# 16-bit projections, the first pair's values and the dilation-4 table loaded beside the last projection job, and another order between the two mixers of a Hymba-style encoder block

## The chip, the cores and the metric

The kernel runs on one core of one Trainium2 chip. The metric is the device time of one execution in microseconds. TensorE (PE) multiplies matrices, VectorE (DVE), ScalarE (ACT) and GpSimd (POOL) work on elements, and SyncE (SP) issues most DMAs.

## The reference

One encoder block over 2048 tokens of 1024 numbers, in float32. What matters here is its first half:

```python
h = rmsnorm(x, g_attn_norm[l])
proj = h @ w_in[l]                     # 1024 -> 3*512 + 256 + 128 + 32
q_a, k_a, v_a, c_q, c_kv, k_rope = jnp.split(proj, splits, axis=-1)
out_a = mixer_dilated(heads(q_a), heads(k_a), heads(v_a), rel_bias)   # 8 heads of 64
out_b = mixer_mla(c_q, c_kv, k_rope, g_q_latent[l], w_q_up[l], g_kv_latent[l], w_kv_up[l])
```

`mixer_dilated` attends in three windows, with keys 1, 4 and 16 tokens apart and a bias by distance for each, and joins them by their softmax denominators. `mixer_mla` is attention over low-rank latents. Behind it come the output projection with a residual, a mixture of 32 experts, and a last norm; the change does not touch these.

## The kernel before

**Number format.** Each projection is computed three times over: both operands are split into a high part and the residual (`hT_hi`, `hT_lo`; `w_hi`, `w_lo` or `wc_hi`, `wc_lo`), and hi x hi, lo x hi and hi x lo are summed in PSUM. The parts are fp32r, a 32-bit format that TensorE takes as it is; the trace prints its matmuls as f32. `split` (L98) does it with one ScalarE copy and one VectorE subtraction.

**Phase 1** (L83). `stage_a` norms a tile of 128 tokens, `stage_b` transposes it on TensorE into `hT`, and `stage_c` multiplies it with the 416 latent columns (24 matmuls). The loop over 16 tiles also lets helpers (Python generators) advance a step at a time: `bias_tables` (L410) builds the bias tables from one-hot matrices, which it keeps in the last 768 columns of `hT_hi`, and `vscale` (L229) finds a power of two by which v fits fp16: Squares of the weights, a ones-matmul that sums over partitions (L350), and some ten tiny VectorE operations (`pow2_scale`, L344). `gmax` is the largest g_attn.

Then come six jobs. The two "v" jobs do 16 tiles of 256 columns each (L309, evicted at L316). The four "qk" jobs do 8 groups each of 24 matmuls of 512 tokens (L329); each group is evicted as an fp16 high part and its residual (`qk_sb`, L339 and L340, two buffers each) and stored to DRAM by two DMAs on SP (L342). At the start of each job the weights of the next are split, with `qkscale` for its scale; `v_copies` makes rearranged copies of v in DRAM (`v1`, `v1e`, `v4`, `v4e`) beside the qk jobs. At the start of the last job `pre3` (L456) asks for head 0's q and k and for the bias tables `t16` and `t1` (the page calls all tables t).

**Phase 3** (L513), the dilated attention, loads the values of head pair 0 (L545) and the table `t4` (L579), scales the three tables on GpSimd (`scale_tables`, L572), and goes through 160 steps: scores on TensorE (L645), `soft1` on VectorE (L670), `soft2` on GpSimd (L687), the exponential on ScalarE (L697), transposes on TensorE (L710), then the product with v.

**mla_prep** (L1006) prepares mixer B: its weights `wkv` are split, `stage_a1` norms a tile's latents (L1036), `stage_a2` transposes them, `stage_b` multiplies and writes the values `VB` (L1079). `qk_scales` (L793) finds the scale of its scores by a ones-matmul (L799) and a VectorE chain.

The order on each engine is that in which the code is written; waits are set by what reads and writes which buffer. PSUM tile `pm` has four buffers.

## Time and the profile before

| | us |
|---|---|
| median of 3 executions | 2322.38 (2321.01 to 2323.44) |
| the profiled execution | 2328.61 |
| its span, first to last instruction | 2326.8 |
| TensorE / VectorE / ScalarE / GpSimd busy in it | 2077.9 / 1653.5 / 1426.9 / 1093.3 |

The profiled execution's time stands 1.8 us above its span: that is what lies around the first and last instruction. Busy times are those of the hardware profiler. In the rows further below a row of a timeline begins with its start and its length in us; "x8" are instructions taken together, and the bracket gives how long the engine stood idle before and what ended that. The mean granted clock of TensorE was 0.948 of its full rate.

### The profile page before, as it was taken

The numbers are of one execution on the slowest core, as the hardware profiler recorded it, in microseconds if no ns is written. First come the engines' busy times: TensorE is split into PE (matmuls) and PEld (weight loads), VectorE is DVE, ScalarE is ACT, GpSimd is POOL, SyncE is SP. The second block draws the span as 40 slices with busy tenths as digits, with TensorE's granted clock in tenths as the row PEclk, the third lists the DMA queues.
The fourth block names the chain that finished last, engine by engine and source line by source line (L and its number), as shares of the span: only waits on it lengthen the run. The fifth ranks groups of instructions, "written<-read, shape, count | busy, mean of one in ns | idle before, by whom it ended". The sixth has DMA issues, their size and how long they took to land. (4 is left out here: it accounts for less than half of the span.)

```text
span 2326.8 us, 42792 instructions
## 1 busy us (share of the span) xinstructions
PE 2077.9 (89%) x16087; PEld 1584.7 (68%) x16087; DVE 1653.5 (71%) x3656; ACT 1426.9 (61%) x2121; POOL 1093.3 (47%) x1193
## 2 busy tenths in 40 slices
PE   6899989688988899999999999788888899999990
PEld 5899778577777556656656555477776588788870
DVE  7722221388886888888888899967787677777755
ACT  4522211399996588888888878734443366677653
POOL 1100000278763255555555556644564656776640
PEclk9999999899998899999999999999998999999995
DMA  5412434867735100000000231145544689999978
GB/s 163 126 58 62 144 140 112 178 156 170 160 99 139 48 22 6 22 22 6 22 22 6 45 102 26 34 135 160 151 143 158 205 307 292 293 307 313 305 212 306
DMA packets 196676, 312.81 MB, mean 134 GB/s; under 512 B 64185, under 2 KB 149090, under 8 KB 183460
## 3 DMA queue, kind: packets, MB, share of 16 engines
q1 hardware_dynamic: 166420, 174.43, 26.2%
q0 software_dynamic: 29760, 134.85, 18.0%
q8 instruction: 127, 2.08, 0.4%
q10 hardware_dynamic: 288, 0.79, 0.1%
q14 instruction: 81, 0.66, 0.1%
HBM read 235.66 MB, written 101.25 MB: 145 GB/s over the span
## 5 line engine op out<-in xcount | busy, mean ns | idle before, releaser
L923 POOL TENSOR_TENSOR lo<-p,hi 128x512 f16<-128x512 f32 x256 | 342.7, 1343 | 297.3 <-ACT p L917 235.5
L916 ACT ACTIVATE hi<-S,mla_scale 128x1024 f16<-128x1024 f32 x256 | 285.2, 1114 | 136.2 <-PE S L911 134.7
L885 DVE TENSOR_REDUCE part<-M 128x1 f32<-128x512 f32 x512 | 340.4, 680 | 12.8 <-PE M L883 11.5
L917 ACT ACTIVATE p<-S,mla_scale 128x1024 f32<-128x1024 f32 x256 | 284.8, 1113 | 0.1
L922 DVE TENSOR_TENSOR lo<-p,hi 128x512 f16<-128x512 f32 x256 | 228.7, 894 | 11.3 <-ACT p L917 9.5
L945 PE MATMUL O<-VB,lo 128*128 128x65 f16 x2048 | 198.4, 194 | 7.6 <-DVE lo L922 5.3
L940 PEld LDWEIGHTS <-hi 128*128 128x128 f16 x2048 | 184.6, 98 | 28.0 <-issue 22.7
L940 PE MATMUL O<-VB,hi 128*128 128x129 f16 (+1 forms) x2048 | 198.5, 215 | 0.0
L945 PEld LDWEIGHTS <-lo 128*128 128x128 f16 x2048 | 177.5, 99 | 18.0 <-DVE lo L922 6.4
L693 POOL TENSOR_TENSOR pp<-sb,st 128x256 f32<-128x256 f32 (+1 forms) x256 | 142.6, 579 | 43.3 <-DVE st L670 30.5
L572 POOL TENSOR_SCALAR t<-t,a_scale 128x512 f32<-128x512 f32 (+1 forms) x12 | 16.1, 1351 | 305.1 <-DMA t<-d_r 290.9
L2077 DVE TENSOR_TENSOR s<-raw,s 128x1024 fp32r<-128x1024 f32 x120 | 140.2, 1221 | 15.0 <-ACT s L2075 13.8
L2121 POOL DMA_INDIRECT d_x<-o,rec x47 | 94.0, 2000 | 107.3 <-ACT s L2075 35.5
L710 PE MATMUL PT<-ident,pp 128*128 128x128 f32 (+1 forms) x640 | 104.3, 287 | 43.8 <-ACT pp L697 41.5
L2034 PE MATMUL pd<-s,hT 128*128 128x512 f32 x540 | 138.2, 404 | 1.7 <-ACT hT L2021 1.7
L1385 PE MATMUL pm<-s,mT_hi 128*128 128x512 f32 x512 | 136.1, 413 | 3.8 <-ACT mT_hi L1370 3.8
L340 DVE SCALAR_TENSOR_TENSOR qk_sb<-pm,qkscale,qk_sb 128x512 f16<-128x512 f32 x32 | 23.9, 750 | 152.5 <-ACT qk_sb L339 152.5
L697 ACT ACTIVATE pp<-pp,a_scale 128x512 f32<-128x512 f32 (+1 forms) x160 | 113.8, 711 | 29.3 <-POOL pp L687 19.8
L2075 ACT ACTIVATE s<-raw 128x1024 fp32r<-128x1024 f32 x120 | 118.3, 1050 | 11.5 <-DMA raw<-in_w_up,eidx 4.7
L2034 PEld LDWEIGHTS pd<-s,hT 128*128 128x128 f32 x540 | 101.2, 188 | 30.1 <-issue 4.3
L339 ACT ACTIVATE qk_sb<-pm,qkscale 128x512 f16<-128x512 f32 x32 | 21.9, 687 | 161.8 <-PE pm L329 110.4
L1385 PEld LDWEIGHTS pm<-s,mT_hi 128*128 128x128 f32 x512 | 98.1, 197 | 26.0 <-ACT mT_hi L1370 4.1
(502 smaller groups left out, 6081.2 us busy)
## 6 DMA issues: line engine op xcount, KB each, us to landing
x<-in_x SPq DMA_DIRECT2D x32, 512.0 KB
na<-d_na SPq DMA_DIRECT2D x48, 264.0 KB
d_qk<-qk_sb SPq DMA_DIRECT2D x64, 128.0 KB
d_x<-x SPq DMA_DIRECT2D x16, 512.0 KB
d_h<-h SPq DMA_DIRECT2D x16, 512.0 KB
y<-d_x SPq DMA_DIRECT2D x16, 512.0 KB
out<-y SPq DMA_DIRECT2D x16, 512.0 KB
d_q<-qs SPq DMA_DIRECT2D x16, 384.0 KB
```

The lines of the kernel that those rows point to most:

```text
L693: nc.gpsimd.tensor_sub(dst, src, res[:, s0 + i, 65:66, None, None].to_broadcast([128, 2, na, nx // 2]))
L885: nc.vector.tensor_reduce(part[m][:, qt, kc:kc + 1], ps, axis=AX.X, op=ALU.max)
L916: nc.scalar.activation(hi, ps, AF.Exp, scale=es)
L917: nc.scalar.activation(p32, ps, AF.Exp, scale=es)
L922: nc.vector.tensor_sub(lo[:, :, 0:LV], p32[:, :, 0:LV], hi[:, :, 0:LV])
L923: nc.gpsimd.tensor_sub(lo[:, :, LV:512], p32[:, :, LV:512], hi[:, :, LV:512])
L940: nc.tensor.matmul(o[:, c0:c0 + own], hi[:, j, q], V[:, 0:own], start=(kt == 0 and qt == 0), stop=False, skip_group_check=True)
L945: nc.tensor.matmul(o[:, c0:c0 + 65], lo[:, j, q], V[:, 0:65], start=False, stop=(kt == 15 and qt == 3), skip_group_check=True)
L1385: nc.tensor.matmul(ps[half], mT[a][:, j], wo[b][j // 2][:, j % 2, 512 * half:512 * half + 512], start=(n == 0), stop=(n == 23))
L2034: self.nc.tensor.matmul(ps[:, half], hT[a][:, j], w[b][:, j, 512 * half:512 * half + 512], start=(n == 0), stop=(n == len(k) - 1))
L2075: nc.scalar.activation(hi, src, AF.Copy)
L2077: eng.tensor_sub(lo, src, hi)
```

## The change

(1) `hT`, `wc` and the split weights are fp16. As fp16 reaches less far than fp32r, the operands are multiplied by powers of two before the split and the results by the inverse on eviction: `xs` for h comes from gmax at the very start, and `weight_scale` gives one for each weight block (`wsc`). The latent weights' scale needs a Square over both halves ahead of the first split. `vscale` and `qkscale` get a second ones-matmul and chain each, and `qkscale` runs whole at the job's start. (2) The one-hot matrices have a tile of their own. (3) `pre3` also makes room for the first pair's values and `t4`; a generator `ahead3` asks for them, a step in each group of the last job, and only `t16` is scaled ahead of the first attention step, `t1` and `t4` at steps 1 and 9. (4) In `mla_prep` the split of `wkv` stands behind the first `stage_a2`, its Square behind the second, and `qk_scales` behind the second `stage_b`.

The diff, cut to what bears on this:

```diff
-            hT = [hp.tile([128, 8, S], F32R, name="hT_hi"), hp.tile([128, 8, S], F32R, name="hT_lo")]
+            hT = [hp.tile([128, 8, S], F16, name="hT_hi"), hp.tile([128, 8, S], F16, name="hT_lo")]
+
+            xs = hp.tile([128, 2], F32, name="hscale")
+            wsc = [hp.tile([128, 3], F32, name=f"wscale{i}") for i in range(3)]
...
-            def split(hi, lo, src):
-                nc.scalar.activation(hi, src, AF.Copy)
-                nc.vector.tensor_sub(lo, src, hi)
+            def split(hi, lo, src, sc):
+                nc.scalar.activation(hi, src, AF.Copy, scale=sc)
+                nc.vector.scalar_tensor_tensor(lo, src, sc, hi, op0=ALU.mult, op1=ALU.subtract)
+
+            def weight_scale(am, w, out):
+
+                nc.vector.memset(am[:, 2:3], 1.0)
+                yield from self.pow2_scale(sm, pt, am, 1.0, w[:, 0:1], None, w[:, 1:2])
+                nc.vector.tensor_scalar(w[:, 2:3], w[:, 1:2], xs[:, 1:2], out, op0=ALU.mult, op1=ALU.mult)
...
-                split(wcv[0][:, 4 * h:4 * h + 4], wcv[1][:, 4 * h:4 * h + 4], wraw[h])
+                split(wcv[0][:, 4 * h:4 * h + 4], wcv[1][:, 4 * h:4 * h + 4], wraw[h], wsc[2][:, 0:1])
...
+            am = sm.tile([128, 4], F32, name="vmax")
+            nc.vector.tensor_reduce(am[:, 2:3], gb, axis=AX.X, op=ALU.max, apply_absolute_value=True)
+            nc.vector.tensor_copy(gmax, am[:, 2:3])
+            self.pow2(sm.tile([128, 8], F32, name="p2"), gmax, gmax, float(D), xs[:, 0:1], xs[:, 1:2])
             stage_a(0)
+            am = sm.tile([128, 4], F32, name="vmax")
+            for h in range(2):
+                nc.scalar.activation(wcv[h][:, 0:4], wraw[h], AF.Square, accum_out=am[:, h:h + 1])
+            list(weight_scale(am, wsc[2], 1.0))
             split_c(0)
             stage_b(0)
             split_c(1)
...
-                nc.vector.tensor_reduce(am[:, 2:3], gb, axis=AX.X, op=ALU.max, apply_absolute_value=True)
-                nc.vector.tensor_copy(gmax, am[:, 2:3])
-                nc.vector.tensor_copy(self.mam[:, 5:6], am[:, 2:3])
+                nc.vector.tensor_copy(am[:, 2:3], gmax)
+                nc.vector.tensor_copy(self.mam[:, 5:6], gmax)
                 yield
                 yield from self.pow2_scale(sm, pt, am, float(D), vsc, dr["va_inv"])
+                a2 = sm.tile([128, 4], F32, name="vmax")
+                nc.vector.tensor_copy(a2[:, 0:2], am[:, 0:2])
+                yield from weight_scale(a2, wsc[0], vsc)
...
+                yield from weight_scale(a2, wsc[g % 2 + 1], s2[:, 0:1])
...
-            tables = self.bias_tables(rawp, hT[0][:, :, 1280:2048], tb)
+            tables = self.bias_tables(rawp, xp.tile([128, 4, 768], F32R, name="onehot", bufs=1), tb)
...
-                if c in (10, 11, 12, 13, 14):
+                if c >= 9:
                     next(vs, None)
+                    if c >= 13:
+                        next(vs, None)
...
                     self.pre3()
+                    a3 = self.ahead3()
                 if i + 1 < len(jobs):
                     if jobs[i + 1][0] == "qk":
-                        qs_steps = qkscale(i + 1)
-                        next(qs_steps)
+                        for _ in qkscale(i + 1):
+                            pass
...
-                        nc.scalar.activation(vt[:, :, 0:64], pv, AF.Copy, scale=vsc)
-                        nc.vector.scalar_tensor_tensor(vt[:, :, 65:129], pv, vsc, vt[:, :, 0:64],
+                        nc.scalar.activation(vt[:, :, 0:64], pv, AF.Copy, scale=wsc[0][:, 2:3])
...
+                            if i == len(jobs) - 1:
+                                next(a3, None)
+                            s2 = wsc[g % 2 + 1][:, 2:3]
...
+        self.pre2 = self.c_pre.enter_context(tc.tile_pool(name="p3pre2", bufs=1, side="right"))
+        self.c_v = ExitStack()
+        pv = self.c_v.enter_context(tc.tile_pool(name="p3pv", bufs=1, side="right"))
+        self.v0 = lambda: pv.tile([128, 63, 2, VW], F16, name="v0")
+        self.t4 = pv.tile([128, 8, 256], F32, name="t4")
...
+    def load_v(self, p, t):
+
+        nc, dr = self.nc, self.dram
+        R = 8 * VW
+        f = t.rearrange("p b h n -> p b (h n)")
+        for n, b0, nb, src in ((128, 0, 16, "va"), (128, 16, 15, "v1"), (96, 31, 4, "v1e"), (128, 35, 12, "v4"), (96, 47, 16, "v4e")):
+            nc.sync.dma_start(f[:n, b0:b0 + nb], AP(dr[src], p * 2 * VW, [[R, n], [n * R, nb], [1, 2 * VW]]))
+            if src != "v1":
+                yield
+
+    def ahead3(self):
+
+        nc, dr = self.nc, self.dram
+        self.v_first = self.v0()
+        yield from self.load_v(0, self.v_first)
+        for a in range(4):
+            nc.sync.dma_start(self.t4[32 * a:32 * a + 32].rearrange("p h (a x) -> p (h a) x", a=4),
+                              AP(dr["r4"], a * 3072, [[1, 32], [96, 32], [1, 64]]))
+            yield
 
...
-            def scale_tables(g):
-                for t in (t16, t1, t4):
+            def scale_tables(g, ts):
+                for t in ts:
                     nc.gpsimd.tensor_scalar(t[:, 2 * g:2 * g + 2], t[:, 2 * g:2 * g + 2], self.asc[:, g, 0:1], None, op0=ALU.mult)
 
-            t4 = tp.tile([128, 3072], F32, name="t4")[:, 0:2048].rearrange("p (h x) -> p h x", h=8)
-            vl = load_v(0)
-            next(vl)
-            next(vl)
-            for a in range(4):
-                nc.sync.dma_start(t4[32 * a:32 * a + 32].rearrange("p h (a x) -> p (h a) x", a=4),
-                                  AP(dr["r4"], a * 3072, [[1, 32], [96, 32], [1, 64]]))
-            list(vl)
-            scale_tables(0)
+            t4 = self.t4
+            vs[0] = self.v_first
+            scale_tables(0, (t16,))
...
+                    if s in (1, 9):
+                        scale_tables(0, (t1,) if s == 1 else (t4,))
...
-        nc.scalar.activation(wkv[1][:, :, 0:64], raw2[:, :, 0:64], AF.Square, scale=gkv, accum_out=self.mam[:, 2:3])
-        nc.scalar.activation(wkv[0], raw2, AF.Copy, scale=gkv)
-        nc.vector.scalar_tensor_tensor(wkv[1], raw2, gkv, wkv[0], op0=ALU.mult, op1=ALU.subtract)
...
-        self.qk_scales(self.sm4, pt)
         stage_a2(0)
+        nc.scalar.activation(wkv[0], raw2, AF.Copy, scale=gkv)
+        nc.vector.scalar_tensor_tensor(wkv[1], raw2, gkv, wkv[0], op0=ALU.mult, op1=ALU.subtract)
         for c in range(NT):
             if c + 2 < NT:
                 stage_a1(c + 2)
             if c + 1 < NT:
                 stage_a2(c + 1)
+            if c == 0:
+                nc.scalar.activation(raw2[:, :, 0:64], raw2[:, :, 0:64], AF.Square, scale=gkv, accum_out=self.mam[:, 2:3])
             stage_b(c)
+            if c == 1:
+                self.qk_scales(self.sm4, pt)
```

Three places where the order of instructions on an engine differs. First, ScalarE at the start of the program (`raw` holds the halves of the latent weights, `xn` a tile of x, `pT` its transposes). Before:

```order
L141 ACTIVATE xn,ss<-x 128x1024
L99 ACTIVATE wc_hi<-raw 128x1664
L187 ACTIVATE c_junk,mla_norms<-raw 128x128
L160 ACTIVATE hT_hi<-pT 128x4x128 x2
L99 ACTIVATE wc_hi<-raw 128x1664
L187 ACTIVATE c_junk,mla_norms<-raw 128x128
```

After the change:

```order
L150 ACTIVATE xn,ss<-x 128x1024
L207 ACTIVATE wc_hi,vmax<-raw 128x1664
L207 ACTIVATE wc_lo,vmax<-raw 128x1664
L102 ACTIVATE wc_hi<-raw,wscale_114 128x1664
L196 ACTIVATE c_junk,mla_norms<-raw 128x128
L102 ACTIVATE hT_hi<-pT,hscale 128x4x128 x2
L102 ACTIVATE wc_hi<-raw,wscale_114 128x1664
L196 ACTIVATE c_junk,mla_norms<-raw 128x128
```

Two Squares (L207) now stand ahead of the first cast of the weights, and both casts read the scale that comes of them. Second, SP's queue of DMAs in the last projection job (`t_...<-d_t` is t1, `qk_sb` are the stores of the groups, `v` the values of the first pair, `t_...<-d_r_66` is t4). Before, t1 is followed by the sixteen stores, and at their end stands:

```order
L342 DMA d_qk<-qk_sb_3445 128x512
L342 DMA d_qk<-qk_sb_3446 128x512
L545 DMA v<-d_va 128x16x260
L545 DMA v<-d_v_59 128x15x260
L545 DMA v<-d_v1e 96x4x260
L579 DMA t_3485<-d_r_66 32x32x64 x4
L545 DMA v<-d_v_61 128x12x260
L545 DMA v<-d_v4e 96x16x260
```

After the change, from t1 on:

```order
L500 DMA t_3301<-d_t_65 8x8x256 x16
L508 DMA v_3353<-d_va 128x16x260
L367 DMA d_qk<-qk_sb_3355 128x512
L367 DMA d_qk<-qk_sb_3356 128x512
L508 DMA v_3353<-d_v_59 128x15x260
L508 DMA v_3353<-d_v1e 96x4x260
L367 DMA d_qk<-qk_sb_3388 128x512
L367 DMA d_qk<-qk_sb_3389 128x512
L508 DMA v_3353<-d_v_61 128x12x260
L367 DMA d_qk<-qk_sb_3420 128x512
L367 DMA d_qk<-qk_sb_3421 128x512
L508 DMA v_3353<-d_v4e 96x16x260
```

The five loads of v stand ahead of the stores of the first four groups, in one of them two together; the four loads of t4 stand likewise, one ahead of the stores of each of the last four groups. Behind the stores there is nothing left to load for the first pair. Third, ScalarE between the mixers, from the last results of the dilated attention (`st`) on (`t` holds the weights of wkv, `wq_raw` the latents of the first tiles, `css` their norms). Before:

```order
L752 ACTIVATE st_8241<-O 128x4x65
L1025 ACTIVATE s_9377,mla_norms<-t_8854,glat 128x8x64
L1026 ACTIVATE s_9377<-t_8854,glat 128x1024
L1036 ACTIVATE cn<-wq_raw,css 128x256
L1037 ACTIVATE cn<-wq_raw,css 128x128
L1036 ACTIVATE cn<-wq_raw,css 128x256
L1037 ACTIVATE cn<-wq_raw,css 128x128
L1048 ACTIVATE cqT_hi<-pT 128x256
```

After the change, from the second tile's norms on:

```order
L1071 ACTIVATE cn<-wq_raw,css 128x256
L1072 ACTIVATE cn<-wq_raw,css 128x128
L1083 ACTIVATE cqT_hi<-pT 128x256
L1084 ACTIVATE s_9493<-pT 128x128
L1150 ACTIVATE s_9495<-t_8972,glat 128x1024
L1071 ACTIVATE cn<-wq_raw,css 128x256
L1072 ACTIVATE cn<-wq_raw,css 128x128
L1083 ACTIVATE cqT_hi<-pT 128x256
L1084 ACTIVATE s_9493<-pT 128x128
L1158 ACTIVATE t_8972,mla_norms<-t_8972,glat 128x8x64
L1104 ACTIVATE qs<-pq 128x8x64
L1114 ACTIVATE VB<-pv,vb_scale 128x8x64
```

The Square (with the tile that sums it, `mla_norms`) and the split of wkv stood first; now two tiles' norms (L1071, L1072) and the first tile's transposes stand ahead of the split, and the Square stands just ahead of the first tile's results.

## Rows read from the trace of the kernel before

**Rows 1.** The page: busy us, share of the span, instructions by engine.

```profile
PE 2077.9 (89%) x16087; PEld 1584.7 (68%) x16087; DVE 1653.5 (71%) x3656; ACT 1426.9 (61%) x2121; POOL 1093.3 (47%) x1193
```

**Rows 2.** Windows: length; PE, PEld, DVE, ACT, POOL busy; clock; DMA share; GB/s.

```profile
30.00:92.00 62.00, 55.48 (x283) 48.88 (x282) 45.07 (x133) 26.96 (x75) 9.54 (x48) 0.92 0.38 111
...
233.00:383.00 150.00, 140.28 (x588) 114.15 (x589) 29.29 (x70) 26.44 (x36) 0.00 (x0) 0.94 0.36 130
...
394.00:404.00 10.00, 10.00 (x45) 8.21 (x44) 0.47 (x1) 0.00 (x0) 0.93 (x1) 1.00 0.60 79
...
428.00:436.00 8.00, 1.59 (x26) 1.29 (x23) 2.62 (x24) 1.18 (x3) 0.00 (x0) 0.81 1.01 250
436.00:444.00 8.00, 0.00 (x0) 0.00 (x0) 0.00 (x0) 0.00 (x0) 0.00 (x0) 0.50 1.34 178
```

**Rows 3.** Timeline of the start.

```profile
9.32 1.59 ACT L99 ACTIVATE wc_hi<-raw 128x1664 fp32r<-128x1664 f32 x1 [2.02 <-DMA raw<-in_w_in]
...
12.83 1.75 PE L168 MATMUL pm<-wc_hi,hT_hi 128*128 128x416 f32 x4
```

**Rows 4.** Timeline of VectorE, tiles 12 and 13: maximum; first and last of a chain.

```profile
113.55 1.21 DVE L235 TENSOR_REDUCE vmax<-g_attn 128x1 f32<-128x1024 f32 x1
...
128.21 0.15 DVE L352 COPY p<-pT 128x2 f32<-128x2 f32 x1
...
129.68 0.14 DVE L364 TENSOR_SCALAR p<-p 128x1 int32<-128x1 int32 x1
```

**Rows 5.** Timeline of TensorE in the loop over tiles.

```profile
48.99 0.42 PE L434 MATMUL pT<-hT_hi 33*8 33x496 f32 x1 [0.98 <-ACT hT_hi L160]
...
95.19 1.77 PE L168 MATMUL pm<-wc_hi,hT_hi 128*128 128x416 f32 x8
...
99.83 1.03 PE L158 MATMUL pT<-ident,xn 128*128 128x128 f32 x8
...
115.67 0.58 PE L350 MATMUL pT<-vmax,ones 128*128 128x2 f32 x2 [3.93 <-DVE hT_lo L161]
```

**Rows 6.** Timeline of TensorE in mixer B, 16-bit operands.

```profile
899.69 0.38 PE L910 MATMUL S<-Ql,Kh 96*128 96x512 f16 x1
...
900.56 0.38 PE L910 MATMUL S<-Ql,Kh 96*128 96x512 f16 x1
```

**Rows 7.** Timeline of ScalarE: evictions of value and q/k jobs.

```profile
201.21 0.47 ACT L316 ACTIVATE v_sb<-pm,va_scale 128x256 f16<-128x256 f32 x1 [2.25 <-PE pm L309]
...
252.13 0.69 ACT L339 ACTIVATE qk_sb<-pm,qkscale 128x512 f16<-128x512 f32 x1 [4.81 <-PE pm L329]
...
332.14 0.69 ACT L339 ACTIVATE qk_sb<-pm,qkscale 128x512 f16<-128x512 f32 x1 [7.38 <-DMA d_qk<-qk_sb]
...
410.96 1.27 ACT L339 ACTIVATE qk_sb<-pm,qkscale 128x512 f16<-128x512 f32 x2 [17.28 <-DMA d_qk<-qk_sb]
```

**Rows 8.** Timelines of TensorE, SP and GpSimd from the last job on.

```profile
381.81 1.99 PE L329 MATMUL pm<-hT_hi,wc_hi 128*128 128x512 f32 x8
...
388.27 15.24 SPq L467 DMA_DIRECT2D t<-d_t  x16
...
427.48 0.22 PE L645 MATMUL S<-KA,QA 128*128 128x128 f16 x1 [1.56 <-DVE qk_sb L340]
...
446.38 1.56 POOL L572 TENSOR_SCALAR t<-t,a_scale 128x512 f32<-128x512 f32 x1 [33.74 <-DMA t<-d_r]
447.90 4.06 POOL L687 TENSOR_TENSOR pp<-sb,st 128x512 f32<-128x512 f32 x4
...
449.76 1.11 PE L710 MATMUL PT<-ident,pp 128*128 128x128 f32 x4 [19.93 <-ACT pp L697]
```

**Rows 9.** Timelines of ScalarE and TensorE between the mixers.

```profile
706.01 0.72 ACT L1025 ACTIVATE s<-t,glat 128x512 fp32r<-128x512 f32 x1 [6.48 <-DMA d_na<-st]
...
706.88 0.60 PE L799 MATMUL pT<-mla_norms,ones 128*128 128x6 f32 x2 [7.77 <-ACT s L1025]
...
716.56 0.69 ACT L1079 ACTIVATE VB<-pv,vb_scale 128x512 f16<-128x512 f32 x1 [0.52 <-PE pv L1066]
```

More of the change, by code (lines that the diff above doesn't have):

```diff
@@ L125, in phase1 @@
             nc.scalar.dma_start(gb, AP(io["g_attn_norm"], 0, [[0, 128], [1, D]]))
-            wc = [wp.tile([128, 8 * 416], F32R, name="wc_hi"), wp.tile([128, 8 * 416], F32R, name="wc_lo")]
+            wc = [wp.tile([128, 8 * 416], F16, name="wc_hi"), wp.tile([128, 8 * 416], F16, name="wc_lo")]
             wcv = [t.rearrange("p (j n) -> p j n", j=8) for t in wc]
@@ L171, in stage_c @@
                 cj = cev.tile([128, 256], BF16, name="c_junk")
-                nc.scalar.activation(cj, ps[:, 0:256], AF.Square, accum_out=self.css[:, 0, c:c + 1])
-                nc.scalar.activation(cj[:, 0:128], ps[:, 256:384], AF.Square, accum_out=self.css[:, 1, c:c + 1])
+                o = wsc[2][:, 2:3]
+                nc.scalar.activation(cj, ps[:, 0:256], AF.Square, scale=o, accum_out=self.css[:, 0, c:c + 1])
+                nc.scalar.activation(cj[:, 0:128], ps[:, 256:384], AF.Square, scale=o, accum_out=self.css[:, 1, c:c + 1])
                 cs = cev.tile([128, 416], F32, name="c_sb")
-                nc.scalar.activation(cs, ps[:, :416], AF.Copy)
+                nc.scalar.activation(cs, ps[:, :416], AF.Copy, scale=o)
                 t = cev.tile([128, 4, 16], F32, name="c_rope")
@@ L212, in split_job @@
                     if 0 not in sps:
-                        sps[0] = [sps["pool"].tile([128, 2048], F32R, name="w_hi"),
-                                  sps["pool"].tile([128, 2048], F32R, name="w_lo")]
+                        sps[0] = [sps["pool"].tile([128, 2048], F16, name="w_hi"),
+                                  sps["pool"].tile([128, 2048], F16, name="w_lo")]
                     w = sps[0]
@@ L219, in split_job @@
                 r = raws.pop(i)
+                sc = wsc[0 if kind == "v" else g % 2 + 1][:, 0:1]
                 if kind == "v":
-                    split(w[0], w[1], r)
+                    split(w[0], w[1], r, sc)
                 else:
@@ L249, in qkscale @@
                 s2 = sq[g % 2]
+                a2 = sm.tile([128, 4], F32, name="vmax")
+                nc.vector.tensor_copy(a2[:, 0:2], am[:, 0:2])
                 yield from self.pow2_scale(sm, pt, am, float(D), s2[:, 0:1], None, s2[:, 1:2], low=16.0)
+                yield from weight_scale(a2, wsc[g % 2 + 1], s2[:, 0:1])
                 a = self.asc[:, g]
@@ L334, in phase1 @@
                                 next(vc, None)
-                            if hh == 0 and n4 in (1, 3):
-                                next(qs_steps, None)
-                            s2 = sq[g % 2][:, 0:1]
+                            if i == len(jobs) - 1:
+                                next(a3, None)
+                            s2 = wsc[g % 2 + 1][:, 2:3]
                             qs = [qkp.tile([128, 512], F16, name=f"qk_sb{t}") for t in range(2)]
@@ L367, in pow2_scale, with pow2 @@
         yield
+    def pow2(self, m, u, v, k, scale, inv, low=1e-30):
+        V = self.nc.vector
+        V.scalar_tensor_tensor(m[:, 0:1], u, k, v, op0=ALU.mult, op1=ALU.mult)
+        V.tensor_scalar(m[:, 1:2], m[:, 0:1], low, 1e30, op0=ALU.max, op1=ALU.min)
+        mi = m.bitcast(I32)
+        V.tensor_scalar(mi[:, 1:2], mi[:, 1:2], 1, None, op0=ALU.logical_shift_right)
+        V.tensor_scalar(mi[:, 1:2], mi[:, 1:2], float(127 << 22), None, op0=ALU.add)
+        V.tensor_single_scalar(mi[:, 2:3], mi[:, 1:2], 0x7F800000, op=ALU.bitwise_and)
+        V.tensor_scalar(scale.bitcast(I32), mi[:, 2:3], -1.0, float((127 + 14 + 127) << 23), op0=ALU.mult, op1=ALU.add)
+        V.tensor_scalar(mi[:, 3:4] if inv is None else inv.bitcast(I32), mi[:, 2:3], -float(14 << 23), None, op0=ALU.add)
     def v_copies(self):
@@ L540, in load_v @@
             def load_v(p):
-                R = 8 * VW
-                t = vp.tile([128, 63, 2, VW], F16, name="v")
-                f = t.rearrange("p b h n -> p b (h n)")
-                def ld(np_, b0, nb, src):
-                    nc.sync.dma_start(f[:np_, b0:b0 + nb], AP(src, p * 2 * VW, [[R, np_], [np_ * R, nb], [1, 2 * VW]]))
-                vs[p] = t
-                ld(128, 0, 16, dr["va"])
-                yield
-                ld(128, 16, 15, dr["v1"])
-                ld(96, 31, 4, dr["v1e"])
-                yield
-                ld(128, 35, 12, dr["v4"])
-                ld(96, 47, 16, dr["v4e"])
+                t = vs[p] = self.v0() if p % 2 == 0 else vp.tile([128, 63, 2, VW], F16, name="v")
+                for _ in self.load_v(p, t):
+                    pass
             def vblk(pat, w, half):
@@ L772, in phase3 @@
                     if u == 5 and h % 2 == 0 and h // 2 + 1 < 4:
-                        list(load_v(h // 2 + 1))
+                        load_v(h // 2 + 1)
                     if u == 12 and h % 2 and h // 2 + 1 < 4:
-                        scale_tables(h // 2 + 1)
+                        scale_tables(h // 2 + 1, (t16, t1, t4))
+                    if s in (1, 9):
+                        scale_tables(0, (t1,) if s == 1 else (t4,))
                     qk(s)
```

28 lines of the change are left out of this document (8 added, 20 removed).

## The prediction

> **What bounds the kernel now.** I read the page first, then the busy times by stretch, then the timelines of the stretches that the diff touches. TensorE is busy 2077.9 us, 89% of the span [rows 1], so in most places what counts is how long its stream is and where it stands still. The stretch table shows which is which: from 233 to 383 us it is busy 94% of the time, VectorE and ScalarE less than a quarter of it; in 394 to 404 it never rests, with the DMA engines 60% busy; from 436 to 444 no compute engine does anything, the DMA engines are full and the granted clock is 0.50, which is 1.2 of 2.4 GHz [rows 2]. So there are four kinds of ground: a start ruled by loads and ScalarE, a projection loop in which TensorE, ScalarE and VectorE take turns, projection jobs ruled by TensorE's stream, and two transitions ruled by waits.
>
> **1. The start.** Before, ScalarE casts the first half of the latent weights at 9.32 (1.59 us); the first projection matmul starts at 12.83 [rows 3], and the matmuls of the second half wait for a second cast. Now a scale has to be known first: two Squares over the halves (1.6 us each by the cast's row, same size and engine), a ones-matmul, and a VectorE chain. The chain of the same code runs from 128.21 to 129.82, 1.6 us, and a ones-matmul pair takes 0.58 [rows 4, 5]. So 2 x 1.6 + 0.2 read + 0.6 + 1.6 + three small operations at about 0.15 with their hand-overs (0.4) = 6.0. I take 0.7 off, because the first tile's hT was made between the cast and the matmul, and its transposes now stand ready early: **+5.3** (both halves alike). Bounds: +3, if the wait for the next x tiles that follows absorbs half; +7, if each hand-over between engines costs as much as the 0.98 seen below. The gain's maximum over g_attn (1.21 us, [rows 4]) moves from tile 12 to here; it lies beside the loads.
>
> **2. The loop over 16 token tiles.** A tile's 24 matmuls of 416 columns take 4.64 us (95.19 to 99.83), 193 ns each [rows 5]. The nearest 16-bit rows are in the latent attention: 512-column matmuls start 0.217 us apart (899.69 to 900.56, four in 0.87) [rows 6], 0.424 ns a column. For 416 columns that gives an estimate of 0.176, 4.23 a tile, 0.41 less; over 15 tiles -6.1. I take -4: TensorE is busy only 89% in this loop (55.48 of 62, [rows 2]), so ScalarE's and VectorE's part of a tile, a little longer than before (the residual becomes a scaled subtraction), will soon be the longer one. The one-hot tables stood in hT_hi, and two of their matmuls waited 0.98 each for ScalarE's hT_hi, the first at 48.99 [rows 5]; with a tile of their own: -2. The maximum moved away takes -1.2 from the 3.93 us hole ahead of 115.67 [rows 4, 5], and the half clock behind such holes shrinks a little: -1.6. Against that a second ones-matmul for the value weights stands in TensorE's order at tile 13, behind VectorE's chain of 1.6 and the residuals ahead of it: +3.3, between 1.6 (the chain alone) and 3.93 (the hole seen). Sum **-5.5**, bounds -10 to 0.
>
> **3. The value jobs.** 32 tiles, one each 2.25 + 0.47 = 2.72 us by the eviction's rows, which wait for TensorE [rows 7]. With 0.424 x 256 = 0.1085 a matmul, 24 take 2.60: 32 x 0.12 = **-3.7**; 0 to -4.5.
>
> **4. The q/k jobs.** A group of 24 matmuls of 512 columns takes 4.81 + 0.69 = 5.50 [rows 7], and 24 x 0.217 = 5.21 as 16-bit: 0.29 each. The first three jobs have 24 groups: -6.9. In the last groups of the second job, evictions wait 7.38 us for earlier stores (ACT at 332.14, [rows 7]) because the copies of v fill the DMA engines; there a faster TensorE only waits longer, so I give back 1.7: -5.2. At each job's start the scale chain is now run whole, with two ones-matmuls, while TensorE stands: the second waits only for one copy, 0.15 and two hand-overs, +0.35 at four starts, +1.4. The cast of the weights waits some 4 us longer on ScalarE, and evictions queue behind it; that is hidden while four PSUM buffers take TensorE's groups (4 x 5.2 us). Sum **-3.8**, 0 to -8.
>
> **5. Last job and the start of dilated attention.** The largest term. Before, the last job starts on TensorE at 381.81, its SP queue holds q/k of head 0, the tables t16 and t1 (16 loads, 15.24 us to 403.5) and then the 16 stores; the third eviction waits 17.28 us for a store [rows 7, 8]. TensorE runs on into its free PSUM buffers, and ends at 425.9. Only then are v of the first pair and t4 asked for; GpSimd waits 33.74 us for t4, scales it at 446.38, its first step of attention starts at 447.90, and TensorE goes on at 449.76 after 19.93 us of rest [rows 8]. So the first GpSimd step of attention is 66.1 us after the job's start.
>
> After, v and t4 are asked for between the stores, and attention starts with t16 alone scaled, t1 and t4 at steps 1 and 9. The 20 us wait is gone, if the job ends as early. It can't quite: v is 3.9 MB; in 428 to 436 the engines move 250 GB/s, full, so it takes some 13 to 15 us, and t4, 1 MB at 178 GB/s [rows 2], 6. That is some 19 us of full DMA which now stands ahead of or between stores. A store can't land before the load issued ahead of it, and an eviction needs the store two before it (two buffers). By the same waits as before, the third eviction comes at about 35 us after the job's start (29.1 before, plus the first 1.06 MB piece of v and its neighbour), so TensorE's seventh group, which needs that PSUM buffer, starts at 35 instead of 31; the remaining five evictions follow at the pace of the loads between them, 3 to 4 us each, the last at about 52. q/k of step 0, VectorE's and GpSimd's start follow 1.9 later, as 427.48 was 1.56 behind the job's end, and GpSimd a little more: 53.9. **-12.** Bounds: -21 if the stores are not held up at all (8 x 5.21 + 0.7 + 0.9 + 1.9 = 45.2); -3 if all 19 us stand behind the third eviction's 29.1 and three evictions with their stores follow them at 5 us.
>
> The Trainium skill, "DMA: Bandwidth & Descriptors", section "Queues, rings and completion order", says that each of the 16 engines takes the descriptors of a row's ring in order, so stores behind loads wait for them. The 17.28 us row agrees. By the rule the term is -12, by free passage -21.
>
> **6. Between the mixers.** Before, ScalarE's first step of mixer B waits 6.48 us for stores of mixer A (706.01), TensorE waits 7.77 for it (706.88), the scales follow, and the first value block VB is written at 716.56 [rows 9]. The rows of the new order put the latent norms, their transposes and the first projections ahead of that; these use loads that are long there. VB itself lies where the last stores read, so it stays behind them, at about 707 instead of 716.56. The Square and the scale chain come back at tiles 0 and 1, beside TensorE's work, some 1.5 in all: **-8**; bounds -11 (nothing comes back) and -3 (only the chain is hidden).
>
> **Sum:** 5.3 - 5.5 - 3.7 - 3.8 - 12 - 8 = -27.7. The profiled execution took 2328.6, the median is 2322.4; the difference is in no stretch that is touched, so I take it off the median: **2295 us**. Out projection and experts keep their code.
>
> **Rivals.**
> A. *The loads hide entirely*: stores slip between, term 5 is -21: 2322.4 - 36.7 = 2286. For it: DMA is only 60% busy while t1 loads [rows 2]. Against: the 17.28 us wait. Chance 0.20.
> B. *The collision is worse*: the seventh and eighth groups starve and attention starts at 63: 2322.4 - 18.7 = 2304. For it: the rows of a full DMA, 1.0 to 1.3 [rows 2]. Chance 0.15.
> C. *16 bits bring nothing*: TensorE takes as long for a 16-bit as for the old column here, since stationary blocks are loaded as often; the terms 2 to 4 lose 4 + 3.7 + 5.2 = 13: 2308. Against: [rows 6], each with a stationary block of its own. Chance 0.08.
> D. *Slower*: TensorE gets the half clock in the 16-bit jobs, as it does from 436 to 444 in its rest. Each us so run costs half a us; 55 us of the 245 us of jobs would cancel the sum, 65 would make it slower by 0.2%, all of them give 2322.4 - 27.7 + 122 = 2417. Against: [rows 6] at full pace in the same format, and a busy TensorE in the jobs. Chance 0.03.
>
> **The numbers.** Forecast 0.54, own range 2289 to 2301. The range 2279 to 2312 takes in A, B and C. No change is what 0.2% (4.6 us) can't tell. Faster: forecast, A, B, and C for the most part: 0.93; same 0.04 (start at its upper bound, mixers and transition at their small ones); slower 0.03.
>
> **What would show it.** Right: first projection matmul near 18.1; value evictions 2.60 apart, q/k evictions 5.2; no matmul of the tables behind hT_hi; an eviction in the last job that waits for a store; the first attention exponential some 54 us after the job's start; VB near 707 less what came before. Wrong: evictions 2.72 and 5.5 apart as before (C), a clock of 0.5 in the jobs (D), the last job's evictions in even steps of 5.2 (A), or TensorE idle over 10 us between its last group and attention (B). What I know least is how stores and loads share the queue in the last job, 18 us between its bounds.

## The result and the profile after

The changed kernel takes 2309.3 us (median of 6 runs, 2304.1 to 2312.8), the one before 2321.7 beside it: ratio 0.9944, 95% interval 0.9924 to 0.9965. So it is faster, by about 13 us, less than half of the forecast 27.7. Ratios are of undisturbed executions alone; two of the ten of one kernel below, the 16-bit format alone, took 3390 and 4890 us at granted clocks of 0.57 and 0.43 and stand in none. The page of the changed kernel's profiled execution begins:

```profile
span 2310.6 us, 42905 instructions
```

Before, the span was 2326.8, 16.2 us more. Where they come from is read from the starts of seven pieces of work in the two timelines:

| start of | before | after | piece before it, forecast | measured |
|---|---|---|---|---|
| first projection matmul | 12.83 | 18.26 | +5.3 | +5.43 |
| first value job | 135.90 | 150.63 | -5.5 | **+9.30** |
| first q/k job | 233.79 | 241.62 | -3.7, starts +0.7 | -6.90 |
| last job | 381.81 | 384.99 | -5.2, starts +0.7 | -4.65 |
| first GpSimd step of attention | 447.90 | 441.09 | -12 | -9.99 |
| last exponential of attention | 695.78 | 692.07 | 0 | +3.10 |
| first value block of mixer B | 716.56 | 702.66 | -8 | -10.19 |

The pieces sum to -13.9; behind them another 2.3 us are gone in this execution. One piece is far off and of the wrong sign, by 14.8 us, which is the whole of what is missing: the loop over 16 token tiles. Its end on TensorE:

```profile
106.05 1.95 PE L167 MATMUL pT<-ident,xn 128*128 128x128 f32 x8 [4.71 <-DVE hT_lo L103]
...
116.83 0.59 PE L375 MATMUL pT<-vmax,ones 128*128 128x2 f32 x2 [2.93 <-DVE hT_lo L103]
...
127.56 0.66 PE L167 MATMUL pT<-ident,xn 128*128 128x128 f32 x4 [2.57 <-DVE hT_lo L103]
131.47 0.56 PE L375 MATMUL pT<-vmax,ones 128*128 128x2 f32 x2 [3.26 <-DVE vmax L107]
...
141.69 0.66 PE L167 MATMUL pT<-ident,xn 128*128 128x128 f32 x4 [2.57 <-DVE hT_lo L103]
...
150.63 1.04 PE L336 MATMUL pm<-w_hi,hT_hi 128*128 128x256 f16 x8
```

Five holes (stretches in which TensorE stands idle) of 2.57 to 4.71 us in 45, where the old loop had two at this place, 3.93 [rows 5] and 2.15:

```profile
126.28 0.66 PE L158 MATMUL pT<-ident,xn 128*128 128x128 f32 x4 [2.15 <-DVE hT_lo L161]
```

The first one begins with ScalarE, whose first Square over the value weights waits for their load:

```profile
101.18 1.91 ACT L252 ACTIVATE hT_hi<-raw 128x2048 f16<-128x2048 f32 x1 [6.25 <-DMA raw<-in_w_in]
```

Before, the same Square stood one tile later and waited 0.93:

```profile
98.81 1.92 ACT L233 ACTIVATE hT_hi<-raw 128x2048 fp32r<-128x2048 f32 x1 [0.93 <-DMA raw<-in_w_in]
```

Windows over the end of the loop (columns as in rows 2) show that holes also cost clock: 0.52 and 0.51 of the full rate, about its 1.2 GHz level, behind the holes that end at 116.83 and 131.47. Behind the last one, at 141.69, the clock stayed full.

```profile
97.00:150.60 53.60, 37.56 (x182) 20.96 (x180) 21.93 (x71) 23.80 (x51) 7.77 (x36) 0.84 0.24 80
116.00:123.00 7.00, 6.17 (x19) 2.97 (x20) 4.61 (x15) 0.81 (x2) 0.80 (x5) 0.52 0.08 30
130.00:137.00 7.00, 5.53 (x18) 2.73 (x19) 1.12 (x10) 0.00 (x0) 0.00 (x0) 0.51 0.04 2
142.00:149.00 7.00, 7.00 (x43) 4.00 (x42) 2.31 (x12) 3.04 (x7) 0.76 (x5) 1.00 0.08 32
```

The jobs go as worked out: ScalarE's evictions come 2.62 apart in the value jobs (2.15 + 0.48 and 2.14 + 0.47 in turn) where it was 2.72 before, and 4.49 + 0.69 = 5.18 in the q/k jobs (5.50), except where stores are late, which they are for longer (23.13 instead of 17.28 us in the last job, [rows 7]):

```profile
180.63 0.48 ACT L341 ACTIVATE v_sb<-pm,wscale 128x256 f16<-128x256 f32 x1 [2.15 <-PE pm L336]
...
253.86 0.69 ACT L364 ACTIVATE qk_sb<-pm,wscale 128x512 f16<-128x512 f32 x1 [4.49 <-PE pm L354]
...
419.37 0.69 ACT L364 ACTIVATE qk_sb<-pm,wscale 128x512 f16<-128x512 f32 x1 [23.13 <-DMA d_qk<-qk_sb]
```

The first attention step, and TensorE behind it, no longer wait 20 us for t4 [rows 8], though TensorE waits 6.15 us for the last eviction:

```profile
441.09 4.07 POOL L723 TENSOR_TENSOR pp<-sb,st 128x512 f32<-128x512 f32 x4 [23.48 <-DVE st L706]
...
438.85 0.27 PE L681 MATMUL S<-KA,QA 128*128 128x128 f16 x1 [6.15 <-DVE qk_sb L365]
...
442.95 1.11 PE L746 MATMUL PT<-ident,pp 128*128 128x128 f32 x4 [0.52 <-ACT pp L733]
```

Between the mixers TensorE goes on at once, and VB still waits for stores [rows 9]:

```profile
696.27 1.31 PE L1080 MATMUL pT<-ident,cn 128*128 128x128 f32 x6 [0.87 <-ACT cn L1071]
...
702.66 0.69 ACT L1114 ACTIVATE VB<-pv,vb_scale 128x512 f16<-128x512 f32 x1 [1.33 <-DMA d_na<-st]
```

### The profile page after: what moved, and what is told of

Same layout as the page of the kernel before. It is cut to its first block, busy times and chain, and to the rows that moved or that the text cites. A ratio compares the mean times of both kernels' runs of the same rounds, so it can differ in the third digit from the quotient of the medians.

```text
span 2310.6 us, 42905 instructions
## 1 busy us (share of the span) xinstructions
PE 2060.5 (89%) x16099; PEld 1458.3 (63%) x16099; DVE 1666.5 (72%) x3741; ACT 1439.9 (62%) x2125; POOL 1092.7 (47%) x1193
## 5 line engine op out<-in xcount | busy, mean ns | idle before, releaser
L2161 POOL DMA_INDIRECT d_x<-o,rec x47 | 88.1, 1874 | 106.7 <-ACT s L2115 33.7
L365 DVE SCALAR_TENSOR_TENSOR qk_sb<-pm,wscale,qk_sb 128x512 f16<-128x512 f32 x32 | 24.0, 750 | 149.3 <-ACT qk_sb L364 149.3
L364 ACT ACTIVATE qk_sb<-pm,wscale 128x512 f16<-128x512 f32 x32 | 22.0, 688 | 153.4 <-DMA d_qk<-qk_sb 76.8
```

## The experiments

Ratios are to the kernel before, from runs beside it on the same chip, with 95% intervals; the changed kernel's is 0.9944. An interval is some 4 to 7 us wide each way, so small differences are read from starts in the timelines. These stand for one execution each and vary too: with the same code up to there, tile 10 starts at 97.0 to 99.5 in twelve kernels, and the first value job at 147.8 to 151.6 in seven. All diffs are against the changed kernel.

**The loop over tiles.** First the value scale one tile later:

```diff
-                if c >= 9:
+                if c >= 10:
                     next(vs, None)
-                    if c >= 13:
+                    if c >= 12:
```

> The changed kernel, but the scale of the value weights starts at tile 10 instead of tile 9 and takes two steps a tile from tile 12 on, so that it still ends at tile 14. Theory: in the changed kernel the first Square over the value weights stands one tile nearer to the load that it reads and waits 6.25 us for it (101.18), which opens a hole of 4.71 us on TensorE ahead of tile 11; with the later start the hole is gone, the first value job starts at about 146 instead of 150.6, and the whole is 4 to 5 us shorter than the changed kernel. Rival: the loop over tiles is longer because the 16-bit split costs ScalarE and VectorE more per tile; then the wait only changes its name, and the first value job still starts within 1 us of 150.6.

The first value job starts at 146.58, 4.05 earlier, although tile 10 began 2.4 later in this execution (99.36 against 96.96); ratio 0.9921 (0.9890 to 0.9952), which can't be told from the changed kernel's. The Square no longer waits, and the hole that it opened ahead of tile 11 is gone; the other four stay:

```profile
102.31 1.92 ACT L252 ACTIVATE hT_hi<-raw 128x2048 f16<-128x2048 f32 x1
...
113.46 0.59 PE L375 MATMUL pT<-vmax,ones 128*128 128x2 f32 x2 [3.75 <-DVE hT_lo L103]
...
123.73 0.66 PE L167 MATMUL pT<-ident,xn 128*128 128x128 f32 x4 [2.57 <-DVE hT_lo L103]
127.64 0.56 PE L375 MATMUL pT<-vmax,ones 128*128 128x2 f32 x2 [3.25 <-DVE vmax L107]
...
137.64 0.66 PE L167 MATMUL pT<-ident,xn 128*128 128x128 f32 x4 [2.57 <-DVE hT_lo L103]
```

Then one sum for both scales:

```diff
-                yield from self.pow2_scale(sm, pt, am, float(D), vsc, dr["va_inv"])
-                a2 = sm.tile([128, 4], F32, name="vmax")
-                nc.vector.tensor_copy(a2[:, 0:2], am[:, 0:2])
-                yield from weight_scale(a2, wsc[0], vsc)
+                yield from self.pow2_scale(sm, pt, am, float(D), vsc, dr["va_inv"], w=wsc[0])
+                nc.vector.tensor_scalar(wsc[0][:, 2:3], wsc[0][:, 1:2], xs[:, 1:2], vsc, op0=ALU.mult, op1=ALU.mult)
...
+        if w is not None:
+            m2 = sm.tile([128, 8], F32, name="p2w")
+            self.pow2(m2, m[:, 7:8], self.ones[:, 0:1], 1.0, w[:, 0:1], w[:, 1:2])
         self.pow2(m, m[:, 7:8], m[:, 6:7], k, scale, inv, low)
```

(and the same in `qkscale`)

> The changed kernel, but the weights' own scale for the value and q/k jobs is worked out from the sum that the first ones-matmul already gives, so that the second ones-matmul (and its PSUM buffer pT) falls away, in the loop over tiles and at the four job starts. Theory: of the loop's 14.8 us over the forecast the second ones-matmul has 3.26 (its own wait for VectorE), 2.57 (transposes of the next tile wait for a pT buffer) and some 3 of half clock behind these holes; the first value job starts at about 142 instead of 150.6, the four job starts give 0.4 each, and the whole is 8 to 10 us shorter than the changed kernel. Rival: only its own wait counts, since the other two come from the first ones-matmul anyway: 3 to 5 us.

First value job at 141.16, 9.47 earlier, ratio 0.9890 (0.9863 to 0.9918). Two holes are gone, the second ones-matmul's own and one in the next tile's transposes:

```profile
106.26 1.31 PE L167 MATMUL pT<-ident,xn 128*128 128x128 f32 x8 [2.68 <-DVE hT_lo L103]
...
117.02 0.58 PE L372 MATMUL pT<-vmax,ones 128*128 128x2 f32 x2 [3.92 <-DVE hT_lo L103]
...
127.14 0.66 PE L167 MATMUL pT<-ident,xn 128*128 128x128 f32 x4 [2.57 <-DVE hT_lo L103]
```

Whether the four job starts gain as well can't be told: from the first value job to the last job it takes 232.5 us here, and 232.7 to 234.7 in the nine kernels that keep both ones-matmuls. Both edits together:

> The two edits to the value scale together (it starts at tile 10, and one ones-matmul serves both scales). Theory: they take away different holes (4.7 us ahead of tile 11; 3.3 and 2.6 us with their half clock behind tiles 12 and 13), so their gains at the first value job add up: 150.6 - 4.1 - 9.5 = 137, against 135.9 before the change, and the whole comes to about 2293, ratio 0.987. Rival: both shift the same waits for VectorE, and together they give no more than the one sum alone: first value job at 141.

The first value job starts at 135.63: 15.0 earlier, where 13.5 were expected, and where the forecast had put it (135.9 + 5.3 - 5.5 = 135.7). Ratio 0.9885 (0.9864 to 0.9907); the time can't be told from that of the one sum alone, the starts can. Two of the five holes are left:

```profile
111.68 0.58 PE L372 MATMUL pT<-vmax,ones 128*128 128x2 f32 x2 [4.21 <-DVE hT_lo L103]
...
121.60 0.66 PE L167 MATMUL pT<-ident,xn 128*128 128x128 f32 x4 [2.57 <-DVE hT_lo L103]
```

Last, the value scale's ones-matmul takes its PSUM buffer from the pool of the bias tables, `self.pow2_scale(sm, tb, ...)` instead of `pt`:

> The later value scale with one sum, and its ones-matmul in the PSUM pool of the bias tables, which is idle by then. Theory: the hole of 2.57 us that remains behind tile 13 is the second half of a tile's transposes waiting for one of two pT buffers, which the ones-matmul holds; with a buffer of its own for it the hole closes and the first value job starts 2.5 to 4 us earlier, at 132 to 133 instead of 135.6. Rival: VectorE is late with hT_lo for reasons of its own (the chain that it has to run), and the hole only moves: within 1 us of 135.6.

First value job at 127.61, 8.0 earlier than with the two edits, twice what was expected; ratio 0.9842 (0.9812 to 0.9872). Not only the hole of 2.57 us but also most of the 4.21 ahead of the ones-matmul was a wait for a pT buffer; what is left there is 0.86, a wait for the second Square:

```profile
108.74 0.38 PE L372 MATMUL pT<-vmax,ones 128*128 128x2 f32 x2 [0.86 <-ACT hT_hi L252]
```

From tile 11 to the first value job it takes 25.0 us, where the changed kernel took 42.8. In the window with tile 10 TensorE is busy 29.23 of 30.10 us, at its full clock:

```profile
97.50:127.60 30.10, 29.23 (x180) 17.90 (x179) 21.31 (x67) 22.95 (x49) 8.03 (x36) 1.00 0.42 138
```

Counted between starts inside the loop, which leaves out how late tile 10 began, the three edits stand clear of one another in the changed kernel and all twelve runs of this section:

| piece (before the change) | kernels | us |
|---|---|---|
| tile 10 to tile 11 (5.4) | scale from tile 9, nine | 8.2 to 11.0 |
| | scale from tile 10, four | 5.1 |
| tile 11 to first value job (35.3) | two ones-matmuls, nine | 41.0 to 42.8 |
| | one sum, two | 33.5 and 33.8 |
| | one sum with a buffer of its own, two | 25.0 and 25.4 |

**The start.** A fixed factor for the latent weights:

```diff
-            for h in range(2):
-                nc.scalar.activation(wcv[h][:, 0:4], wraw[h], AF.Square, accum_out=am[:, h:h + 1])
-            list(weight_scale(am, wsc[2], 1.0))
+            nc.vector.memset(wsc[2][:, 0:1], 1024.0)
+            nc.vector.tensor_scalar(wsc[2][:, 2:3], xs[:, 1:2], 1.0 / 1024.0, None, op0=ALU.mult)
```

> The changed kernel with a fixed factor of 1024 for the latent weights instead of one found from the data: the two Squares, the ones-matmul and the chain at the start are left out, so this kernel does not fit its scale to the weights. Theory: the chain's 5.4 us at the start are carried in full to the end, since TensorE waits again only for what shifts with it: the first projection matmul at about 13, tile 10 and the first value job 5 us earlier, the whole 5 us shorter than the changed kernel. Rival: the loop that follows waits for the loads of x and for VectorE anyway, and takes most of it back: tile 10 less than 2 us earlier.

The first projection matmul starts at 15.28, not 13: 3.0 earlier. The cast of the weights now waits for its factor, which VectorE writes behind the first tile's norm:

```profile
12.68 1.68 ACT L102 ACTIVATE wc_hi<-raw,wscale 128x1664 f16<-128x1664 f32 x1 [5.31 <-DVE wscale L207]
```

That norm begins 1.7 us later than before the change (9.04 against 7.32), since the chain for the scale of h stands ahead of it; the rest of the 2.4 us that stay is the place of this factor. Tile 10 starts at 95.48, 1.5 to 4.0 earlier than in the twelve kernels that keep the chain, the first value job at 146.33, 1.5 to 5.3 earlier than in the seven; ratio 0.9917 (0.9896 to 0.9937). So the 5 us of the theory aren't there to be carried, and how much of the 3.0 reaches the jobs these runs can't tell.

**The last job.** Loads behind the job: `next(a3, None)` is taken out, `list(self.ahead3())` and the scaling of all three tables stand at the start of phase 3.

> The changed kernel with the first pair's values and the dilation-4 table asked for behind the last job, as before the change, and all three tables scaled ahead of the first step. Theory: the loads beside the job are worth what the profile says, 66.1 to 56.1 us from the job's start to the first GpSimd step of attention, so without them the kernel is 8 to 10 us longer than the changed one. Rival: the 16-bit job ends earlier by itself (8 groups at 5.18 instead of 5.50) and the stores do not queue, so most of the 10 us stays: 2 to 5 us longer.

The last job starts at 383.30 and the first GpSimd step at 452.94, 69.6 us later, 13.5 more than in the changed kernel, where the theory had 10, and 3.5 more than before the change; ratio 0.9990 (0.9975 to 1.0005), some 10 us longer than the changed kernel. The wait for t4 is back:

```profile
451.41 1.56 POOL L611 TENSOR_SCALAR t<-t,a_scale 128x512 f32<-128x512 f32 x1 [36.64 <-DMA t<-d_r]
452.94 4.06 POOL L721 TENSOR_TENSOR pp<-sb,st 128x512 f32<-128x512 f32 x4
```

The same loads from ScalarE's queue (`nc.scalar.dma_start` in `ahead3`):

> The changed kernel with the loads of the first pair's values and of the dilation-4 table issued by ScalarE instead of SP. Theory: in the last job the stores wait because they stand behind loads in one queue: with the loads in another queue v starts beside t1, whose 16 loads keep only 0.65 of the DMA engines busy, and the stores stand behind t1 alone: the third eviction waits 17 instead of 23 us, and from the job's start to the first GpSimd step it takes 50 instead of 56 us. Rival: the 16 engines are the limit, whichever queue asks; the same bytes take the same time and the span stays at 54 to 57.

57.8 us from the job's start to the first GpSimd step (56.1 in the changed kernel): no gain, as the rival had it. The store that the third eviction waits for is later still:

```profile
421.13 0.69 ACT L364 ACTIVATE qk_sb<-pm,wscale 128x512 f16<-128x512 f32 x1 [28.33 <-DMA d_qk<-qk_sb]
...
439.35 4.07 POOL L723 TENSOR_TENSOR pp<-sb,st 128x512 f32<-128x512 f32 x4 [16.89 <-ACT QA L585]
```

But the run doesn't take the loads out of SP's way. t1's sixteen loads still stand ahead of the stores there, and SP itself now waits for v before it issues them. SP's waits (us in total, times, longest), then its first store of the job's results, which the changed kernel issues earlier, at 408.67:

```profile
SPq L500 <- DMA v<-d_v: 14.0, 2, 8.7
SPq L564 <- DMA v<-d_va: 5.2, 1, 5.2
```

```profile
414.83 22.98 SPq L367 DMA_DIRECT2D d_qk<-qk_sb  x16
```

```profile
408.67 6.85 SPq L367 DMA_DIRECT2D d_qk<-qk_sb  x2
```

Ratio 0.9914 (0.9894 to 0.9934): if it is shorter, it is not by this; the last job already starts 3.4 earlier, before anything that was edited. The tables a job earlier (t16, t1 and t4 asked for in groups 2 to 7 of the last job but one, all scaled there):

```diff
+                            if i == len(jobs) - 2 and (hh, n4) > (0, 1):
+                                next(et, None)
```

> The changed kernel with the three bias tables loaded during the last job but one, spread over its groups 2 to 7, and scaled ahead of attention; the values of the first pair stay beside the last job. Theory: in the last job the 16 DMA engines are the limit, and t1 is the worst of it, 15 us in which they are only 0.65 busy and the stores stand still; without the tables the last job's loads and stores fit beside its 8 groups, and from the job's start to the first GpSimd step it takes 46 to 49 instead of 56 us, the whole is 7 to 10 us shorter than the changed kernel. Rival: the job before is full too (its first evictions wait for the copies of v), so the loads delay its stores instead: the gain is 3 us or less.

45.0 us instead of 56.1, ratio 0.9877 (0.9844 to 0.9911). SP issues the first store of the job's results at 387.56, 6.8 us after the job's start (23.7 in the changed kernel). The third eviction still waits for a store, but 4.73 us, hardly longer than the 4.49 that it would for TensorE, and the groups run on evenly:

```profile
387.56 5.39 SPq L373 DMA_DIRECT2D d_qk<-qk_sb  x2
...
396.75 0.69 ACT L370 ACTIVATE qk_sb<-pm,wscale 128x512 f16<-128x512 f32 x1 [4.73 <-DMA d_qk<-qk_sb]
...
425.76 4.07 POOL L734 TENSOR_TENSOR pp<-sb,st 128x512 f32<-128x512 f32 x4 [38.41 <-DVE st L717]
```

**Between the mixers.** The old order:

> The changed kernel with the order of before between the two mixers (the Square and split of wkv first, its score scale ahead of the first tile). Theory: the new order is worth 10.2 us (from the last result of the dilated attention to the first value block 17.4 before, 7.2 after), and all of it reaches the end: 10 us longer than the changed kernel. Rival: a part is given back in the later tiles of mixer B, since the score scale comes later: 5 to 8 us longer.

The ratio is the changed kernel's, 0.9944 (0.9927 to 0.9962): neither theory. The first value block starts 14.4 us after the last exponential (688.30), against 10.6 in the changed kernel and 20.8 before. In the old order, then, 6.4 of the 10.2 us are there already, and the wait for the stores is gone from ScalarE; TensorE's first step waits 1.18 instead of 7.77:

```profile
692.80 0.55 PE L837 MATMUL pT<-mla_norms,ones 128*128 128x6 f32 x2 [1.18 <-ACT s L1063]
```

So the buffers of the results were put back as well, `ot = ctx.enter_context(tc.tile_pool(name="p3o", bufs=1))` without `side="right"`:

> The changed kernel with the old order between the mixers and the buffers of the dilated attention's results (st) back on the left side of the memory, as before the change. In the run with the old order alone the wait of 6.48 us for the stores of these results was gone although the order was the old one. Theory: it is the placement of these buffers, not the order, that took that wait away: here it comes back, the time from the last exponential of the dilated attention to the first value block is 20 to 21 us again (14.4 with the old order alone, 10.6 in the changed kernel), and the whole is 6 us longer than with the old order alone. Rival: the wait went because the stores come earlier or faster now; then it stays at 14 to 15.

The wait is back, and the time is 20.8 (690.80 to 711.63); ratio 0.9956 (0.9936 to 0.9977), some 3 us above the old order alone and by itself not to be told from it:

```profile
700.90 0.72 ACT L1063 ACTIVATE s<-t,glat 128x512 fp32r<-128x512 f32 x1 [6.35 <-DMA d_na<-st]
...
711.63 0.69 ACT L1117 ACTIVATE VB<-pv,vb_scale 128x512 f16<-128x512 f32 x1 [0.68 <-PE pv L1104]
```

**The 16-bit format alone**, with the loads, the order and the results' buffers as before:

> The changed kernel with the loads behind the last job, the old order between the mixers and the results' buffers on the left again: what is left of the change is the 16-bit projections with their scales and the tile of their own for the one-hot matrices. Theory: what the jobs gain (11 us up to the last one) is less than what the start (5.4) and the value scale (14) cost, so the 16-bit format alone is 3 to 7 us slower than before, ratio 1.001 to 1.003. Rival, as forecast: its terms 1 to 4 sum to -7.7, ratio 0.997.

Ratio 1.0041 (1.0025 to 1.0058): slower, by about 9 us. Its last job starts 0.8 us later than before, its first GpSimd step 4.6 and its first value block of mixer B 4.7 later. The rest of the 9 us can't be placed: behind that block this profiled execution is 8.2 us shorter than the one before the change.

**All together** (one sum, one tile later, own PSUM buffer, early tables):

> All of these together: value scale one tile later with one sum and a PSUM buffer of its own, tables loaded in the last job but one. Theory: the gains stand one behind the other on TensorE's path and add up: 17 at the first value job, 3 at the later job starts, 8 in the last job, against the changed kernel: about 2281 us, ratio 0.982 to 0.984. Rival: faster groups run into the copies of v, and a third is given back: ratio 0.987.

2269.6 us (2268.7 to 2274.1), ratio 0.9789 (0.9758 to 0.9819), better than the theory's 2281: by the medians 51 us shorter than the kernel before, by the ratios 49, and some 36 shorter than the changed kernel. The first value job starts at 128.70, the first GpSimd step at 404.68, 45.0 after the last job's start.

## Why the prediction was wrong

**Term 2 failed.** Its sum put +3.3 on the second ones-matmul and nothing on the value scale's other steps; measured were +9.30 against -5.5, outside the term's bounds. Three things were left out, and the runs give their sizes. The loop `c >= 9` sends the first Square one tile nearer to its load, which I read as a renumbering of steps: 3.1 to 5.9 between tiles 10 and 11. The second ones-matmul costs not only its own wait, 3.26 as forecast, but holds one of two pT buffers that the next tile's transposes need, 2.57, and behind its wait the clock fell to half: 7 to 9 us in all from tile 11 on, 9.5 at the first value job (one sum alone). Without these two the loop ends where the forecast had it, but that is luck in part. The forecast's -5.5 holds the +3.3 of the second ones-matmul, which that run leaves out: its gains (16 bits, the one-hot tile, the maximum) were put at 8.8 and came to 5.8, 117.3 us from the first projection matmul to the first value job against 123.1 before. I had taken the hole of 3.93 us in the old loop for the price of a reduction and of VectorE. In the new loop the buffer of its own shows that the like hole, 4.21, was PSUM for the most part, and that 8 more us were to be had; for the old loop no run shows it, though place and releaser are the same.

**Term 1** was right in size and in its path: the cast waits for the scale of the latent weights and starts at 15.66 instead of 9.32. What was not seen is that the scale of h makes a second path close behind it, so that taking the first away gives 3.0 and not 5.4.

**Terms 3 and 4** were right in the cadence, 2.62 and 5.18 for 2.60 and 5.21. Their gain was larger by 4, mainly in the second value job, whose start had run at half clock before (from 183.7 for 6.8 us) and did not after. The evictions held up by the copies of v at the end of the second q/k job took back all of that job's gain, not 1.7 us of it: it takes 53.7 us against 52.7 before, though 51.1 to 51.7 in the eight other kernels with the same code in it.

**Term 5** was right in size (-10 for -12) and in what happens, stores behind loads: the third eviction came 34.4 us after the job's start and the last one 52.3, where the sum had 35 and 52. Why the stores wait is shown only in part. Taking the three tables out of the job gave 11 us, and the first store is then issued 6.8 us after the job's start instead of 23.7. Whether the tables cost this by their place in SP's queue, which was my reason, or by the 16 engines stays open. The run from ScalarE's queue was to part the two and does not, since t1 stayed ahead of the stores and SP waited 19.2 us for v. In the changed kernel the engines are busy 0.78 while t1 loads and full behind it:

```profile
391.40:406.90 15.50, 15.50 (x74) 7.02 (x72) 1.19 (x2) 0.69 (x1) 0.93 (x1) 1.00 0.78 135
407.00:424.00 17.00, 12.34 (x52) 5.29 (x51) 0.75 (x1) 0.69 (x1) 1.56 (x1) 0.90 1.11 203
```

The Trainium skill, "DMA: Bandwidth & Descriptors", section "Issuing engines are not separate DMA queues", says that DMAs of all issuing engines run on the same 16 engines, and that a second issuer saves only the time of issuing. That the stretch didn't shorten (57.8 against 56.1 us) agrees with it, but is no test of it for the reason just given.

**Term 6** was right in size (-10.2 for -8) by luck. The order of the code is worth 3.8, with the buffers on the right; 6.4 come from the side of memory on which the results' buffers lie, a word in the diff (`side="right"`) that the prediction passed over. With these buffers on the left ScalarE's Square over the weights of wkv waits for their stores, 6.48 us before the change and 6.35 in the run with the old order and the old side.

**Attention** took 3.1 us longer, which was not forecast. At 553 to 560 the clock fell to half behind a wait of 2.86 us at a change of head pair, where it had not before; between the first GpSimd step and the last exponential the runs took 244 to 251 us with the same code in it, so the runs don't tie it to an edit; why the clock fell in one and not in the other stays open. So do differences of up to 16 us between the first value block and the end (1602.0 to 1617.7 in the runs, 1607.9 in the changed kernel), where the code is the same but for the score scale's place.

Of the rivals, A and B didn't come: the third eviction waits 23.13 us, and TensorE 6.15 ahead of attention, which starts 56.1 after the job's start and not 63. C is out by the cadence. So is D: the mean granted clock of a job was 0.88 to 1.00.

## What to carry to other kernels

When a diff renumbers the steps of a helper that is spread over a loop, write down for each step what it waits for at its old and at its new place, the load asked for a tile earlier first of all. Count PSUM buffers like an engine: a tiny ones-matmul in a pool of two stood in the way of a tile's transposes and made holes of 2.6 and 4.2 us, and a pool that had fallen idle gave 8 us for one word. And ask where each buffer comes to lie, since a wait between two stages may be one for memory and not for data; then look there before the order of the code. Last, before a run is taken for a test of a queue, read what that queue itself waits for.

## What the runs showed of the hardware

A ScalarE operation whose factor is read from a tile took 0.09 us longer than the same without one. The operation that sums the squares of the latents has the same shape and formats in both kernels. Before, then after (busy us, mean ns of one):

```profile
L172 ACT ACTIVATE c_junk<-pm 128x256 bf16<-128x256 f32 x16 | 6.1, 382 | 56.2 <-PE pm L168 56.2
```

```profile
L181 ACT ACTIVATE c_junk<-pm,wscale 128x256 bf16<-128x256 f32 x16 | 7.6, 474 | 52.9 <-PE pm L176 49.6 <-issue 3.3
```

TensorE's clock made short holes dearer than they look: behind holes of 2.93 and 3.26 us it was granted about half its rate over the next 7 us (0.52 and 0.51), and with the holes closed not at all in this stretch. The length of a hole alone doesn't tell: behind the 2.57 us that end at 141.69 the clock stayed at 1.00, and at the start of the second value job a hole of 2.46 us was followed by 0.50 before the change, one of 2.45 by 1.00 after it.
